# Gate and up projections of a SwiGLU block: seven Strassen-Winograd products in another order

## The chip, the cores and the metric

The kernel runs on one core of one Trainium2 chip. The metric is the time of one execution in microseconds (us), taken on the device; smaller is better. Before the change it is 1520.84 us, the median of three runs (1519.15 to 1520.98).

## The reference

One decoder block on 1024 positions of width 1024, in float32. Two mixers (stick-breaking attention and HGRN2) are merged into a residual h; then comes the part that the change touches, a feed-forward network with 2816 hidden channels:

```
hn = rms_norm(h, norm2_g)
ffn = (jax.nn.silu(hn @ w_gate) * (hn @ w_up)) @ w_down
return h + ffn
```

The result must be that of float32 arithmetic.

## The kernel before

Everything is kept transposed: channels lie on the 128 partitions, positions on the free axis, in two halves of 512. A float32 product is made of three matmuls on rounded parts: an operand is split into a high part (a cast, on ScalarE) and a low part (operand minus high part, on VectorE), and high by high, high by low and low by high are summed in one PSUM bank. `full_split` (line 860) issues the two instructions of a split. In the profile the high parts are called oh and the low parts ol.

The hidden channels are 22 tiles of 128. Tile p and tile p + 11 form a pair, and for each of the 11 pairs the gate and then the up are computed. Such a projection is a 2 by 2 block product: two tiles of channels by two halves of positions, with the 1024 input channels cut in two. It is done in Winograd's form with seven block products instead of eight. `left` (line 977) makes the seven left operands from two raw weight tiles, ta = (a11, a12) and tb = (a21, a22), of 512 KB each: operand 1 is a11, 2 is a12, 4 is a22; a21 = a11 - a21 is operand 7; s2 = a22 - a21 is operand 6; a11 = s2 + a11 is operand 5; a12 = a12 - s2 is operand 3. The sums are written back into the raw tiles (called w in the profile) or into s2. The right operands f are made once, earlier. `prod` (line 1002) issues one product: four steps of three matmuls, 12 matmuls in all, into one bank.

`winograd` (line 1028) issues the seven products into three banks and reads the banks in between, so that four output blocks come out: x (in the profile pj) sums products 1 and 2 and is block 0; y (ms) sums 6, 7 and 4; z sums 5 and 3. A copy p1 of product 1 is added to the others on VectorE: c[1] = 6 + 1 + 5 + 3, c[3] = 6 + 7 + 1 + 5, c[2] = 6 + 7 + 4 + 1. A bank that more products are to be added to is read before the next product writes it. For the first gate the order is another (1, 5, half of 2, 6, the channel sums of the norm, 7, rest of 2, 4, 3), since the right operands still come in; for the others it is 1, 6, 5, 7, 2, 4, 3. The blocks are called g in a gate and c in an up. A gate's blocks go through the norm's factor and silu; an up's are multiplied by them, four sums of the products are formed (bs), and all eight are stored for the down stage (act_d). `down_sums` makes four sums of the down weights in the same stage (ds, wd_d).

The instructions of this part are not issued in the order of the code. `Plan` (lines 74 to 211) collects them with a cost each, then goes through time in its own model: whenever an engine is free it takes the ready instruction with the longest way behind it, provided that its buffers have slots, and appends it to that engine's queue. A tile is followed as a whole: whoever writes one half of a raw tile stands in order with whoever reads the other half (lines 102 to 118). Products keep the order of the code (`after=(turn,)`). Loads go through SyncE's queue, in the order that the planner writes. The slots that matter: two raw tiles for a gate (w) and two for an up (wA), four split operands for each (oh and ol; ohA and olA, line 395), three banks each for x and y and two for z. A DMA is counted as landed 2.0 us after its transfer (line 87), a transfer as its KB divided by 350 (line 466).

On the chip each engine runs its queue in order and waits at an instruction until what it needs is there.

After this stage the down stage (from line 1115) multiplies the stored blocks with the down weights in the same form; the last outputs end the kernel.

Of the kernel before, what the change touches and what calls it, by code (L numbers as in the profile page):

```python
# [15 lines left out]
ALU = mybir.AluOpType  # L16
# [198 lines left out]
def hybrid_block(ctx: ExitStack, tc, xT, wi, wb, wo, wg, wu, wd, vec, outT):  # L215
# [213 lines left out]
    def new(ring, shape=(P, HALF), dt=F32):  # L429
        pool, cap, tag, phase = where[ring]  # L430
        plan.ring(ring, cap)

        def make():
            open_pools(phase)
            return (pools[pool] if phase else pool).tile(list(shape), dt, tag=tag, bufs=cap, name=tag)

        return Buf(ring, make, phase)
# [4 lines left out]
    def A(fn, *args, n=HALF, aps=0, rank=0, ps=False, part=False, holds=(), after=(), **kw):  # L442
        us = (0.05 if ps else 0.093) + n / 1200 + 0.0935 * aps
        return plan.op("A", us, [(fn, args, kw)], rank, after, part=part, holds=holds)

    def V(fn, *args, n=HALF, aps=0, rank=0, part=False, holds=(), after=(), **kw):
        cycles = 2 * n if fn == nc.vector.tensor_tensor_scan else n
        us = 0.067 + cycles / 960 + 0.061 * aps
        return plan.op("V", us, [(fn, args, kw)], rank, after, part=part, holds=holds)
# [15 lines left out]
    def L(dst, src, kb, rank=0, after=(), part=False, land=None):  # L465
        return plan.op("D", max(0.47, kb / 350), [(nc.sync.dma_start, (dst, src), {})], rank,
                       after, part=part, land=land)
# [5 lines left out]
    act, tt = nc.scalar.activation, nc.vector.tensor_tensor  # L473
# [40 lines left out]
    def load(dst, src, kb, rank=1):  # L514
        last_load[0] = L(dst, src, kb, rank=rank, after=(last_load[0],))
# [344 lines left out]
    def full_split(src, rings=("oh", "ol"), rank=0):  # L860
        hi, lo = new(rings[0], dt=F32R), new(rings[1], dt=F32R)
        A(nc.scalar.copy, hi, src, rank=rank)
        V(tt, lo, src, hi.bitcast(F32), op=ALU.subtract, rank=rank)
        return hi, lo
# [62 lines left out]
    for i in range(4):  # L927
# [6 lines left out]
        for e in range(2):  # L934
            k = i + 4 * e
            w = get_w(wo[seq.pop(0)])
            for h in range(2):
# [9 lines left out]
                y = new("f" if i < 3 else "y")  # L947
# [29 lines left out]
    def left(src, p, ring):  # L977

        A_ = "A" if ring == "wA" else ""
        sp = lambda t: full_split(t, ("oh" + A_, "ol" + A_))  # L980
        ta, tb = new(ring, (P, 1024)), new(ring, (P, 1024))
        for t, r in ((ta, src[p]), (tb, src[p + NP])):
            if A_:
                last_wu[0] = L(t, r, 512, after=(last_wu[0],))
            else:
                load(t, r, 512, rank=0)
        a11, a12, a21, a22 = ta[:, :512], ta[:, 512:], tb[:, :512], tb[:, 512:]
        s2 = new("s2")
        ops = {1: sp(a11)}
        V(tt, a21, a11, a21, op=ALU.subtract)  # L990
        V(tt, s2, a22, a21, op=ALU.subtract)
        ops[6] = sp(s2)
        V(tt, a11, s2, a11, op=ALU.add)
        ops[5] = sp(a11)
        ops[7] = sp(a21)
        ops[2] = sp(a12)
        ops[4] = sp(a22)
        V(tt, a12, a12, s2, op=ALU.subtract)
        ops[3] = sp(a12)
        return ops  # L1000

    def prod(out, a, p, start, ks=range(4)):

        nonlocal turn
        for k in ks:
            ws = slice(k * P, (k + 1) * P)
            turn = plan.op("P", 0.69, [
                (nc.tensor.matmul, (out, a[p][i][:, ws], fop[p][k][j]),
                 dict(start=start and k == 0 and i + j == 0, stop=k == 3 and i == 1,
                      skip_group_check=True)) for i, j in ((0, 0), (0, 1), (1, 0))], after=(turn,))  # L1010

    def channel_sums():

        nonlocal turn
        ss = []
        for h in range(2):
            hi, lo = new("bs", dt=F32R), new("bs", dt=F32R)
            A(nc.scalar.copy, hi, rs[h])
            V(tt, lo, rs[h], hi.bitcast(F32), op=ALU.subtract)
            ss.append(new("ms"))  # L1020
            turn = M(1024, [(ss[h], ones_r, hi, True, False), (ss[h], ones_r, lo, False, True)],
                     after=(turn,))
        for h in range(2):
            A(act, rs[h], ss[h], AF.Ln, n=HALF + (0 if h else TABLE), ps=True, aps=1, bias=eps_t, scale=1.0 / D)
        for h in range(2):
            A(act, rs[h], rs[h], AF.Exp, n=HALF + (0 if h else TABLE), scale=-0.5)

    def winograd(a, ring, first=False):

        c = [new(ring) for _ in range(4)]  # L1030
        x, y, z, p1 = new("pj"), new("ms"), new("z"), new("p1")
        prod(x, a, 1, True)
        A(nc.scalar.copy, p1, x, ps=True)
        if first:
            prod(z, a, 5, True)
            prod(x, a, 2, False, (0, 1))
            prod(y, a, 6, True)
            channel_sums()
            V(tt, c[1], y, p1, op=ALU.add)
            prod(y, a, 7, False)  # L1040
            prod(x, a, 2, False, (2, 3))
        else:
            prod(y, a, 6, True)
            V(tt, c[1], y, p1, op=ALU.add)
            prod(z, a, 5, True)
            prod(y, a, 7, False)
            prod(x, a, 2, False)
        V(tt, c[3], y, p1, op=ALU.add)
        V(tt, c[3], z, c[3], op=ALU.add)
        prod(y, a, 4, False)  # L1050
        V(tt, c[2], y, p1, op=ALU.add)
        prod(z, a, 3, False)
        V(tt, c[1], z, c[1], op=ALU.add)
        return x, c

    def down_sums(p):
# [10 lines left out]
        for b, t in enumerate((s7, s6, s5, s3)):  # L1067
            L(wdd[p][:, b * HALF:(b + 1) * HALF], t, 256, part=True)

    ag = left(wg, 0, "w")  # L1070
    for p in range(NP):
        au = left(wu, p, "wA")
        x, g = winograd(ag, "g", p == 0)
        V(tt, g[0], x, rs[0], op=ALU.mult)
        for b in range(1, 4):
            V(tt, g[b], g[b], rs[b % 2], op=ALU.mult)
        for b in range(4):
            A(act, g[b], g[b], AF.Silu, n=HALF + (0 if b or p else TABLE))
        for b in range(4):
            V(tt, g[b], g[b], rs[b % 2], op=ALU.mult)  # L1080
        down_sums(p)
        if p + 1 < NP:
            ag = left(wg, p + 1, "w")
        x, c = winograd(au, "c")
        V(tt, c[0], x, g[0], op=ALU.mult)
        for b in range(1, 4):
            V(tt, c[b], c[b], g[b], op=ALU.mult)
        n7, n6, n5, n4 = (new("bs") for _ in range(4))
        V(tt, n7, c[3], c[1], op=ALU.subtract)
        V(tt, n6, n7, c[0], op=ALU.add)  # L1090
        V(tt, n5, c[3], n6, op=ALU.subtract)
        V(tt, n4, c[2], n6, op=ALU.subtract)
        for b, t in enumerate((*c, n7, n6, n5, n4)):
            dst = actd[p][:, b * HALF:(b + 1) * HALF]
            store_a(dst, t) if p == NP - 1 else L(dst, t, 256, part=True)
# [33 lines left out]
    def operands(o, p):  # L1129

        wp = bp = dB
        tags, btags = ("ah", "al"), ("bh", "bl")
        if o == 1 and p < 4:

            rp = wpool if p < 2 else preB
            raw = rp.tile([P, 1024], F32, tag="w", bufs=2, name="w32")
            ra, rb = raw[:, :512], raw[:, 512:]
            if p < 3:
                wp = bp = rp
                tags = btags = ("oh", "ol") if p < 2 else ("ds", "ds")  # L1140
        else:
            ra = dB.tile([P, HALF], F32, tag="ra", name="ra")
            rb = dB.tile([P, HALF], F32, tag="rb", name="rb")
        nc.sync.dma_start(ra, LEFT[o](p))
        nc.sync.dma_start(rb, blk(act_d[p], RIGHT[o]))
        return split(ra, wp, tags) + split(rb, bp, btags)
# [17 lines left out]
    for o in DOWN:  # L1164
        first = o in (1, 6, 5)
        final = o == DOWN[-1]
        for p in range(NP - LAST if final else NP):
            ops = operands(o, p)
# [66 lines left out]
```

## Time and profile before

| | |
|---|---|
| median of three runs | 1520.84 us |
| the profiled execution: its time, its span | 1520.8 us, 1519.1 us |
| granted TensorE clock | 1.00 |
| TensorE busy (matmuls) | 1501.8 us, 99% |
| VectorE busy | 1194.1 us, 79% |
| ScalarE busy | 804.3 us, 53% |
| gate and up, from the first product to the first matmul of the down stage | 874.57 to 1305.93 us |

Times in the rows are microseconds from the start of the span unless they are marked ns. PE is TensorE's matmuls, PEld its weight loads, DVE VectorE, ACT ScalarE, SPq the queue of SyncE, which issues DMAs. A busy PE isn't a PE at its peak: matmuls overlap in the records, so the distance between the starts of two products tells more than the busy time. `out<-in` names what an instruction writes and reads; `[3.34 <-DMA w<-wu]` behind it is the idle time of its engine before it and what ended it. Nearly all instructions have line 194, that of the planner's call, so they are told apart by their tiles.

### The profile page before, as it was taken

How to read it: one execution, taken by the hardware profiler on the slowest of the kernel's cores; microseconds unless marked ns; L12 is line 12 of the kernel's file. 1: busy time of each engine (PE TensorE's matmuls, PEld its weight loads, DVE VectorE, ACT ScalarE, POOL GpSimd, SP SyncE). 2: the span in 40 equal slices, each digit the busy share in tenths (PEclk: the TensorE clock that was granted, in tenths of full speed). 3: DMA queues.
4: the chain of work that ended last, by engine and by line, in shares of the span. 5: the costliest groups of instructions: out<-in, count | busy, mean ns of one | idle time of the engine just before them, and what ended most of it. 6: DMA issues, size and time to landing. Idle time of an engine off the chain costs nothing.

```text
span 1519.1 us, 20504 instructions
## 1 busy us (share of the span) xinstructions
PE 1501.8 (99%) x7213; PEld 1238.3 (82%) x7213; DVE 1194.1 (79%) x2092; ACT 804.3 (53%) x1505; POOL 110.3 (7%) x155
## 2 busy tenths in 40 slices
PE   9999999999999999999999999999999999999999
PEld 6778888888888888888888888777888887888887
DVE  9898789988997877967867798788888888675553
ACT  7867779668758877445434453332332332354442
POOL 4210111211101100110000000000000000000000
PEclk9999999999999999999999999999999999999999
DMA  5111111111111212136434345444445544797662
GB/s 182 40 44 60 54 39 46 44 39 56 51 51 39 68 61 63 51 120 220 163 114 145 112 148 184 150 154 153 163 166 164 161 160 166 256 327 243 199 216 91
DMA packets 83159, 188.53 MB, mean 124 GB/s; under 512 B 9584, under 2 KB 11632, under 8 KB 83056
## 3 DMA queue, kind: packets, MB, share of 16 engines
q1 hardware_dynamic: 72400, 167.82, 34.2%
q10 hardware_dynamic: 10656, 19.40, 3.5%
q8 instruction: 57, 0.93, 0.3%
q14 instruction: 46, 0.38, 0.1%
HBM read 131.61 MB, written 55.57 MB: 123 GB/s over the span
## 4 chain that ended last, share of the span: by engine, by line
PE 69%; DVE 18%; DMA 5%; ACT 4%; issue 3%; POOL 1%; SPq 0%; DVEq 0%; ACTq 0%; POOLq 0%
PE pj L194 34%; PE f L1152 14%; PE ms L194 13%; PE z L194 8%; DVE ol L194 4%; DMA w<-wu 3%; DVE g L194 3%; DMA w<-wg 2%; DVE w L194 2%; DVE c L194 1%; DVE aa L194 1%; ACT aa L194 1%; ACT oh L194 1%; DVE kb L194 1%; DVE bs L194 1%
## 5 line engine op out<-in xcount | busy, mean ns | idle before, releaser
L194 PE MATMUL pj<-ah,oh 128*128 128x512 f32 x704 | 287.2, 408 | 2.4 <-ACT tmp L194 0.9
L194 PE MATMUL pj<-ah,ol 128*128 128x512 f32 x704 | 276.3, 393 | 0.0
L194 PE MATMUL pj<-al,oh 128*128 128x512 f32 x704 | 275.9, 392 | 0.0
L194 ACT CAST oh<-w 128x512 fp32r<-128x512 f32 x164 | 99.6, 619 | 237.3 <-DVE w L194 67.7
L194 DVE TENSOR_TENSOR ol<-w,oh 128x512 fp32r<-128x512 f32 x248 | 170.1, 686 | 31.0 <-ACT oh L194 23.5
L194 PE MATMUL ms<-f,oh 128*128 128x512 f32 x528 | 165.0, 394 | 3.1 <-DVE g L194 2.9
L194 PEld LDWEIGHTS pj<-ah,ol 128*128 128x128 f32 x704 | 132.6, 188 | 29.8
L194 PEld LDWEIGHTS pj<-ah,oh 128*128 128x128 f32 x704 | 132.9, 189 | 26.7 <-DVE aa L194 1.4
L194 PEld LDWEIGHTS pj<-al,oh 128*128 128x128 f32 x704 | 133.1, 189 | 23.1 <-DVE al L194 0.5
L194 PEld LDWEIGHTS ms<-f,oh 128*128 128x128 f32 x528 | 97.5, 188 | 29.5 <-DVE g L194 7.2
L1152 PE MATMUL f<-bh,ah 128*128 128x512 f32 x296 | 115.2, 389 | 0.0
L1152 PE MATMUL f<-bh,al 128*128 128x512 f32 x296 | 115.2, 389 | 0.0
L1152 PE MATMUL f<-bl,ah 128*128 128x512 f32 x296 | 115.1, 389 | 0.0
L194 DVE TENSOR_TENSOR_SCAN aa<-aa,ww 128x512 f32<-128x512 f32 (+3 forms) x96 | 94.2, 996 | 25.3 <-ACT aa L194 14.6
L194 PE MATMUL z<-f,oh 128*128 128x512 f32 x352 | 108.6, 390 | 0.0
L194 PE MATMUL pj<-f,oh 128*128 128x512 f32 x352 | 108.4, 389 | 0.0
L248 DVE TENSOR_TENSOR al<-ra,ah 128x512 fp32r<-128x512 f32 x73 | 50.4, 690 | 70.1 <-ACT ah L247 69.9
L194 PE MATMUL ms<-f,ol 128*128 128x512 f32 x264 | 102.9, 390 | 0.0
L194 POOL TENSOR_SCALAR oh<-w 128x512 fp32r<-128x512 f32 x84 | 68.4, 815 | 437.8 <-PE pj L194 367.7
L247 ACT CAST ah<-ra 128x512 fp32r<-128x512 f32 x73 | 45.5, 624 | 95.6 <-PE f L1152 83.8
L194 PE MATMUL pj<-mx,oh 128*128 128x512 f32 x256 | 78.7, 389 | 0.0
L194 PEld LDWEIGHTS pj<-f,oh 128*128 128x128 f32 x352 | 66.1, 188 | 13.7
(257 smaller groups left out, 3148.7 us busy)
## 6 DMA issues: line engine op xcount, KB each, us to landing
w<-wi SPq DMA_DIRECT2D x42, 512.0 KB, 3.6
rb<-act_d SPq DMA_DIRECT2D x73, 256.0 KB, 4.3
w<-wg SPq DMA_DIRECT2D x22, 512.0 KB, 4.3
w<-wu SPq DMA_DIRECT2D x22, 512.0 KB, 4.5
w<-wd SPq DMA_DIRECT2D x22, 512.0 KB, 5.0
wd_d<-ds SPq DMA_DIRECT2D x44, 256.0 KB, 2.8
ra<-wd_d SPq DMA_DIRECT2D x44, 256.0 KB, 4.1
act_d<-c SPq DMA_DIRECT2D x40, 256.0 KB, 4.2
```

The lines of the kernel that those rows point to most:

```text
L194: fn(*[a.real() if isinstance(a, View) else a for a in args], **{k: v.real() if isinstance(v, View) else v for k, v in kw.items()})
L247: pin(nc.scalar.copy(hi, src))
L248: pin(nc.vector.tensor_tensor(lo, src, hi.bitcast(F32), op=ALU.subtract))
L1152: nc.tensor.matmul(banks[SET[o]][d], l[:, ws], r, start=start and i == 0, stop=p == NP - 1 and i == 2, skip_group_check=True)
```

## The change

The order of products becomes 1, 6, 5, half of 2, 7, the rest of 2, 3, 4; for the first gate 1, 5, half of 2, 6, channel sums, 7, rest of 2, 3, 4. After product 5 its bank is read at once (c[3] = z + p1); the sum of y is added behind product 7. In `left`, the splits of operands 2 and 4 stand in that order too; where two instructions are otherwise equal the planner goes by this order.

```diff
         ops[5] = sp(a11)
+        ops[2] = sp(a12)
         ops[7] = sp(a21)
-        ops[2] = sp(a12)
-        ops[4] = sp(a22)
         V(tt, a12, a12, s2, op=ALU.subtract)
         ops[3] = sp(a12)
+        ops[4] = sp(a22)
         return ops
...
             prod(y, a, 6, True)
             channel_sums()
             V(tt, c[1], y, p1, op=ALU.add)
-            prod(y, a, 7, False)
-            prod(x, a, 2, False, (2, 3))
+            V(tt, c[3], z, p1, op=ALU.add)
         else:
             prod(y, a, 6, True)
             V(tt, c[1], y, p1, op=ALU.add)
             prod(z, a, 5, True)
-            prod(y, a, 7, False)
-            prod(x, a, 2, False)
-        V(tt, c[3], y, p1, op=ALU.add)
-        V(tt, c[3], z, c[3], op=ALU.add)
+            V(tt, c[3], z, p1, op=ALU.add)
+            prod(x, a, 2, False, (0, 1))
+
+        prod(y, a, 7, False)
+        V(tt, c[3], y, c[3], op=ALU.add)
+        prod(x, a, 2, False, (2, 3))
+        prod(z, a, 3, False)
+        V(tt, c[1], z, c[1], op=ALU.add)
         prod(y, a, 4, False)
         V(tt, c[2], y, p1, op=ALU.add)
-        prod(z, a, 3, False)
-        V(tt, c[1], z, c[1], op=ALU.add)
         return x, c
```

## Rows read from the trace of the kernel before

**Rows 1.** The page: span, and busy time, share and instructions of TensorE.
```profile
span 1519.1 us, 20504 instructions
...
PE 1501.8 (99%) x7213; PEld 1238.3 (82%) x7213; DVE 1194.1 (79%) x2092; ACT 804.3 (53%) x1505; POOL 110.3 (7%) x155
```

**Rows 2.** Stretches: first gate, first up, down stage; length, busy time by engine.
```profile
874.57:895.49 20.92, 20.59 (x89) 16.36 (x88) 20.80 (x35) 17.05 (x27) 0.00 (x0) 1.00 0.58 187
895.49:914.53 19.04, 19.04 (x85) 15.77 (x84) 15.87 (x27) 4.92 (x9) 0.00 (x0) 1.00 0.43 149
1305.93:1515.43 209.50, 209.49 (x925) 173.01 (x923) 120.30 (x189) 87.68 (x152) 0.00 (x0) 1.00 0.70 229
```

**Rows 3.** Stretches: products 5 and 7 of the ten later gates; then their sum.
```profile
919.97:925.43 5.46, 5.46 (x25) 4.49 (x24) 4.91 (x9) 1.22 (x2) 0.00 (x0) 1.00 0.81 248
958.59:965.91 7.32, 5.73 (x25) 4.42 (x24) 6.18 (x11) 1.21 (x2) 0.00 (x0) 1.00 0.80 259
999.14:1005.23 6.09, 5.73 (x25) 4.43 (x24) 4.96 (x9) 1.22 (x2) 0.00 (x0) 1.00 0.80 261
...
sum 59.89, PE 57.09 PEld 44.33 DVE 49.18 ACT 12.18 POOL 0.00; mean PE 5.71 PEld 4.43 DVE 4.92 ACT 1.22 POOL 0.00
```

**Rows 4.** Stretches: products 5 and 7 of the ten later ups; then their sum.
```profile
1018.83:1024.81 5.98, 5.88 (x25) 4.35 (x24) 5.48 (x10) 1.28 (x4) 0.00 (x0) 1.00 0.61 166
...
1136.14:1141.75 5.61, 5.61 (x26) 4.19 (x25) 5.10 (x9) 1.08 (x3) 0.00 (x0) 1.00 0.69 187
...
sum 59.21, PE 58.15 PEld 43.41 DVE 53.88 ACT 14.01 POOL 0.00; mean PE 5.81 PEld 4.34 DVE 5.39 ACT 1.40 POOL 0.00
```

**Rows 5.** Waits from 874 to 1306: who, for whom, total us, times, longest.
```profile
DVE w L194 <- DMA w<-wu: 30.6, 10, 4.6
...
PEld ms L194 <- DVE g L194: 7.2, 10, 2.0
PEld z L194 <- DVE ol L194: 4.9, 10, 0.7
...
PEld ms L194 <- DVE c L194: 2.3, 9, 0.3
```

**Rows 6.** VectorE in order of time, one pair: start, us, instruction, [idle before].
```profile
992.49 0.69 DVE L194 TENSOR_TENSOR w<-w 128x512 f32<-128x512 f32 x1 [3.34 <-DMA w<-wu]
...
1001.65 0.68 DVE L194 TENSOR_TENSOR g<-ms,p 128x512 f32<-128x512 f32 x1
1002.25 0.68 DVE L194 TENSOR_TENSOR ol<-w,oh 128x512 fp32r<-128x512 f32 x1
...
1007.86 0.69 DVE L194 TENSOR_TENSOR ol<-w,oh 128x512 fp32r<-128x512 f32 x1 [1.73 <-ACT oh L194]
...
1018.81 0.68 DVE L194 TENSOR_TENSOR ol<-w,oh 128x512 fp32r<-128x512 f32 x1
...
1021.82 0.68 DVE L194 TENSOR_TENSOR ol<-w,oh 128x512 fp32r<-128x512 f32 x1
...
1025.01 0.69 DVE L194 TENSOR_TENSOR c<-ms,p 128x512 f32<-128x512 f32 x1 [0.70 <-PE ms L194]
1025.62 0.68 DVE L194 TENSOR_TENSOR ol<-w,oh 128x512 fp32r<-128x512 f32 x1
```

**Rows 7.** The chain that ended last, two loads of it: start, us to landing.
```profile
987.06 5.41 DMA w<-wu
...
1002.95 4.17 DMA w<-wg
```

**Rows 8.** ScalarE in order of time, the last cast of that up.
```profile
1024.79 0.62 ACT L194 CAST oh<-w 128x512 fp32r<-128x512 f32 x1 [2.21 <-PE ms L194]
```

**Rows 9.** The tile wu: its 22 loads, issue to landing.
```profile
DMA to landing us min/median/max: 3.4/4.5/6.6
```

## The prediction

> **What bounds the kernel now.** The page first: the span is 1519.1 us and TensorE is busy for 99% of it [rows 1], so only lost TensorE time can be won back. The stretches by stage come next. The projections of gate and up run from 874.57 to 1305.93; the down stage behind them is 209.50 us of matmuls without a gap [rows 2], and the change touches nothing before 874. The up of the first pair runs clean: seven products in 19.04 us [rows 2], so a product is 2.72 us, half a product 1.36, and one of its twelve matmuls 0.227. That is the floor; everything above it is what a new order can win.
>
> Where it is lost: product 5 and the product 7 behind it should take 5.44 us together. Over the ten gates after the first they take 59.89 us, 5.49 more than ten times 5.44; in the worst pair 1.88, in a usual one 0.65 [rows 3]. Over the ten ups after the first they take 59.21, or 4.81 more [rows 4]. The first gate takes 20.92; less 19.04 and less four matmuls of channel sums (0.91) that is 0.97 [rows 2]. Together 11.27 us, and that is the most the change can give.
>
> Who is waited for: product 7 on VectorE's c[1] (called g in a gate), which reads the bank that product 7 writes next; product 5 of an up on the low half of its own left operand; and, briefly, product 7 of an up on c[1] [rows 5]. VectorE is late because its queue is in order: at 992.49 it has stood 3.34 us at a21 = a11 - a21, whose raw tile wu came 5.41 us after its issue at 987.06, and from there it takes a step every 0.60 us without a pause [rows 6, 7]. The planner counts 1.46 us for such a load and 2.0 for its landing, 3.46 together (lines 87 and 466), so the queue is written about 2 us too early at that place. The read of c[1] in the gate, due when product 6 ends at 999.14, starts at 1001.65 [rows 3, 6].
>
> **The change, part by part.** No instruction is added or taken: each product keeps its 12 matmuls, the number of VectorE sums stays five in a projection, and z + p1 stands where y + p1 stood, of the same shape. Only order changes, on TensorE, VectorE, ScalarE and, through them, SyncE.
>
> (1) *Half of product 2 goes between 5 and 7.* The read of y into c[1] gets 1.36 us more. Nine of the ten gates lose less than that: 5.49 - 1.88 = 3.61 us together, all of it gone. The worst keeps 1.88 - 1.36 = 0.52. So **-5.0** (bounds -5.5 and 0, where VectorE falls further behind). The cover is 4.08 us behind product 6; if VectorE reaches c[1] later than that, each us is paid once a gate.
>
> (2) *The bank of product 5 is read at once, product 7's sum later.* c[3] = z + p1 goes into VectorE's gap while product 2 runs; when product 7 ends only one sum of two is left, with 4.08 us until product 4 writes that bank (2.72 before). In the first gate the first wait, for c[1] behind the channel sums, stays; the ones behind it, about 0.4 of 0.97, go: **-0.4** (0 to -0.97).
>
> (3) *Product 3 ahead of 4.* c[1] + z, which in the profile comes in the steps behind the late raw tile, is ready one product earlier, and three sums of the output blocks hang on it. The planner places by due time, so one to three steps move from behind the blocked a21 into the 3.34 us that VectorE stands there [rows 6]. I take two, 1.2 us.
>
> (4) *The load behind it moves the other way.* The up has four slots for split operands (ohA, line 395). The planner follows whole tiles (line 105), so the splits of 2 and 5 wait for the sum written back into their tile, while 7 and 4 need only a21: in the up, slots go to 1, 7, 4 and 6, whatever order the lines stand in, and 5, 2 and 3 wait for products to end. The last cast of the up starts at 1024.79, when product 7 ends; its low half follows at 1025.62, and then the next raw tile is issued [rows 6, 8]. Product 7 now ends 1.36 us later within the up, and so does this load of SyncE. Two steps (1.2 us) come back by (3), so c[1] and the gate's raw tiles (wg, 4.17 us [rows 7]) stay where they were. From 1007.86, the first split of the next gate, to 1018.81, the low half of operand 5 of the up, VectorE goes on for 18 steps [rows 6]; the gate's slots also come 1.36 later, so its sums fill the time ahead of that split, and I take two steps fewer, 1.2 us.
>
> So operand 5 of the up: its low half is done at 1018.81 + 0.68 = 1019.49 and was due two matmuls into product 5, at 1018.83 + 0.45 = 1019.28 [rows 4, 6]; 0.2 late, and 0.65 more against a gate that no longer stalls. 0.85 + 1.36 - 1.2 - 1.2 = -0.2: just in time. The wait for c[1] in the up has 1.36 more cover and goes. With loads of 3.4 to 6.6 us [rows 9] some pairs stay late: I keep 1.5 of 4.81, so **-3.3** (bounds -4.8 and +8, where no step is won).
>
> (5) *What is late next.* Operand 2 of the up: its low half starts at 1021.82 [rows 6], done at 1022.50, and is now due two matmuls behind product 5, at 1018.83 + 2.72 + 0.45 = 1022.00. Late by 0.5 where VectorE is as far behind as now, in time when it is 0.6 ahead, as in (4). Operand 3 of the up: product 7 ends, its cast takes 0.6, its low half is done 1.5 us after that end (1024.79 to 1026.30 [rows 6, 8]); due 1.36 + 0.45 = 1.81. In time by 0.3, late by 0.3 with one VectorE step in front. Behind that wait stand the sums of c on VectorE and the raw tile on SyncE. I take half of one miss, 0.15, in eleven ups: **+1.6** (0 to 10, with both late by 0.9 together).
>
> Sum: -5.0 - 0.4 - 3.3 + 1.6 = -7.1 us. The profiled execution took 1520.8 (span 1519.1 and 1.7 around it), the same as the median of the three, 1520.84: **1513.7 us**.
>
> **Rivals.** *A: the wait only moves.* The pitch of a pair is then set by the round of raw tile, VectorE, raw tile, VectorE, not by the read of one bank. For it: between the two waits VectorE has no pause [rows 6], and a gate freed of its stall reaches the up sooner, where operand 5 isn't ready. Against it: in the sixth up the two products take only 5.61 [rows 4], so the round can close within 0.2 of the floor. With two to three steps won instead of four, (4) reads 0.85 + 1.36 - 1.2 (or 1.8) = 0.4 to 1.0 late in an up, with 0.3 for the restart 0.7 to 1.3 a pair, where 1.1 is lost now: -4 to +2 in ten pairs. Time 1520 (1517 to 1523). The Trainium skill has a rule on this side: Perfetto Trace Analysis, section Optimization Strategy, says that one gap repeating through a stretch on the engine that should be full can mean too few buffers for the next tile. By that rule four slots and two raw tiles would decide, the change gives neither, and the time stays. The trace agrees for the up (its casts wait for product ends) and not for the gate, where the wait ends on a read of a PSUM bank.
>
> *B: slower, by the raw tile.* The load in (4) is issued 1.36 us later in every up; if the planner puts no more in front of the blocked a21, all of VectorE's queue shifts by that, and operand 5 of the next up with it. Ten times 1.36 is 13.6 us; less one step in the gate's half, ten times 0.6, leaves +7.6: 1528.4. It decides from the point where fewer than two steps a pair move ahead of a load. For it: that product 7's end starts the cast is in the rows. Against it: the 3.3 us that VectorE stands idle there are room for five steps.
>
> *C: all of it goes.* If four or five steps move, no operand is late, and 11.3 us go less a little for long loads: 1510.0.
>
> **How the numbers follow.** Forecast 0.53 (1511.5 to 1517.5), C 0.18, A 0.18, B 0.11. Under about 0.2%, 3 us, a measurement of this kernel doesn't tell a change from none: faster is below 1517.8, slower above 1523.9. The forecast and C are faster, with a little of A: 0.73; the rest of A and a weak B are within: 0.17; B, and an A with an unlucky operand 3: 0.10. The range leaves out B and the floor: 1509.8 to 1521.0.
>
> **What would show it.** The order on TensorE is pj, ms, z, six matmuls of pj, ms, six of pj, z, ms. (1): no wait of product 7 on c[1] in the gates, or one. (3): the sum c from z stands ahead of a21 in VectorE's queue, and a21 has idled less than 3.3 us. (4): the load of wu behind an up's last cast is issued about 13.7 us (12.24 and 1.5) after that up's first matmul, 12.94 now; product 5 of the ups takes under 2.9 us. (5): a wait of z on a low half at product 3 of the ups under 0.3 us. From one up to the next 38.1 to 38.6 us, now 39.1. I'm wrong if that pitch stays, with the wait at product 5, 2 or 3 of the ups (A), or grows (B).

## The result, and the profile after

The changed kernel takes 1524.05 us (median of 14 runs, 1520.35 to 1528.37), the kernel before 1519.70 (14 runs beside them, 1517.78 to 1523.57): ratio 1.0026, 95% interval 1.0017 to 1.0035. It is slower by about 4 us, 0.3%; 1513.7 was forecast, and the range ended at 1521.0.

The page of the kernel after, span and TensorE, answers to [rows 1]; it counts the same instructions:

```profile
span 1523.0 us, 20504 instructions
...
PE 1499.3 (98%) x7213; PEld 1239.1 (81%) x7213; DVE 1195.0 (78%) x2092; ACT 803.8 (53%) x1505; POOL 112.0 (7%) x155
```

From the first gate to the down stage the trace after goes from 875.18 to 1308.00. Its first stretch is the first gate, its second the first up, as in [rows 2]:

```profile
875.18:895.64 20.46, 20.26 (x89) 16.44 (x88) 20.35 (x34) 16.44 (x26) 0.00 (x0) 1.00 0.60 191
895.64:914.68 19.04, 19.04 (x85) 15.77 (x84) 16.17 (x27) 5.49 (x10) 0.00 (x0) 1.00 0.47 154
```

The first gate has won 0.46. For [rows 3] and [rows 4] the stretch is now product 5, half of 2 and product 7, 6.80 us at the floor (2.72 + 1.36 + 2.72). First come three of the ten later gates of the kernel after, with the sum of all ten; then one of the ten later ups, with the sum of the ten:

```profile
997.84:1004.63 6.79, 6.79 (x31) 5.63 (x30) 5.01 (x9) 1.21 (x2) 0.00 (x0) 1.00 0.73 257
...
1074.09:1083.37 9.28, 7.41 (x32) 5.48 (x30) 8.12 (x14) 1.22 (x3) 0.00 (x0) 1.00 0.60 205
...
1193.89:1203.21 9.32, 7.39 (x32) 5.48 (x30) 8.17 (x14) 1.21 (x3) 0.00 (x0) 1.00 0.58 202
...
sum 80.29, PE 72.03 PEld 55.14 DVE 65.96 ACT 12.21 POOL 0.00; mean PE 7.20 PEld 5.51 DVE 6.60 ACT 1.22 POOL 0.00
```

```profile
1055.06:1061.85 6.79, 6.79 (x31) 5.63 (x30) 6.76 (x12) 1.50 (x3) 0.00 (x0) 1.00 0.36 114
...
sum 67.99, PE 67.99 PEld 56.30 DVE 63.39 ACT 15.07 POOL 0.00; mean PE 6.80 PEld 5.63 DVE 6.34 ACT 1.51 POOL 0.00
```

The ups lose nothing any more. The ten gates lose 80.29 - 68.00 = 12.29, where they lost 5.49 before; 1.55 of it is product 5 in the first two of them, waiting for its own low half. Who is waited for (after, 875 to 1306, columns as in [rows 5]):

```profile
DVE w L194 <- DMA w<-wu: 30.0, 10, 4.5
...
PEld ms L194 <- DVE g L194: 7.1, 8, 1.0
PEld pj L194 <- DVE ol L194: 5.9, 6, 1.7
...
PE pj L194 <- DVE ol L194: 3.6, 4, 1.3
...
PEld z L194 <- DVE ol L194: 1.8, 2, 1.0
```

The two lines of pj are new: the half of product 2 waits for the low half of its operand. Of the eight waits of PEld on g, that is on c[1], six come 1.8 us behind such a wait, in the same gates. TensorE in one such gate (after, order of time: start, us, instruction, [idle before]):

```profile
1076.81 0.61 PE L194 MATMUL pj<-f,oh 128*128 128x512 f32 x2
1078.70 0.50 PE L194 MATMUL pj<-f,ol 128*128 128x512 f32 x1 [1.27 <-DVE ol L194]
...
1080.50 0.73 PE L194 MATMUL ms<-f,oh 128*128 128x512 f32 x2 [0.61 <-DVE g L194]
```

And what VectorE does there (after, same columns):

```profile
1060.21 0.68 DVE L194 TENSOR_TENSOR c<-z,p 128x512 f32<-128x512 f32 x1
...
1069.57 0.69 DVE L194 TENSOR_TENSOR w<-w 128x512 f32<-128x512 f32 x1 [4.47 <-DMA w<-wu]
...
1072.89 0.69 DVE L194 TENSOR_TENSOR c<-z,c 128x512 f32<-128x512 f32 x1
...
1077.96 0.68 DVE L194 TENSOR_TENSOR ol<-w,oh 128x512 fp32r<-128x512 f32 x1
...
1079.16 0.69 DVE L194 TENSOR_TENSOR w<-w,s 128x512 f32<-128x512 f32 x1
1079.76 0.69 DVE L194 TENSOR_TENSOR g<-ms,p 128x512 f32<-128x512 f32 x1
```

The low half at 1077.96 is that of operand 2, since a12 = a12 - s2 at 1079.16 overwrites its tile. Before, in [rows 6], the same step of a gate (the kernel before):

```profile
999.84 0.69 DVE L194 TENSOR_TENSOR ol<-w,oh 128x512 fp32r<-128x512 f32 x1
```

It was done at 1000.52, and in the new order would have been due two matmuls behind product 5, at 999.14 + 2.72 + 0.45 = 1002.31: 1.8 in hand. After, it is done at 1078.64 and due at 1074.09 + 3.17 = 1077.26: 1.4 late.

The wait that ends last is another one. c[1] (the g of 1079.76) is done at 1080.45, 6.36 us after product 6 ended at 1074.09. The new order gives it 4.08, so it is 2.3 late, and 2.33 is what this gate loses ahead of product 7: without the wait for the low half, product 7 would have started no sooner, since VectorE's steps up to c[1] follow each other without a pause. So it is in all six gates that wait at the half of 2, each time to within 0.06 us; the low half is 0.9 less late than c[1]. In [rows 6] c[1] was done at 1002.33, 3.19 after product 6, with a cover of 2.72: 0.5 late. So the cover grew by 1.36, and the time until c[1] is done by 3.2.

Counted from the gate's first matmul (993.70 there, 1068.65 here, two pairs later) the low half has moved from 6.14 to 9.31, and c[1] by as much. Of those 3.2 us, 2.1 lie ahead of a21, which started 1.21 ahead of that matmul and now starts 0.92 behind it, after 4.47 us of idle time where [rows 6] have 3.34. The raw tile it waits for, on SyncE after and as the chain of waits has its load (start, us to landing):

```profile
1058.99 0.33 SPq L194 DMA_DIRECT2D w<-wu  x1
1060.32 1.53 SPq L194 DMA_DIRECT2D w<-wd  x2
1062.12 0.33 SPq L194 DMA_DIRECT2D w<-wu  x1
```

```profile
1062.12 7.42 DMA w<-wu
```

It was 5.41 in [rows 7]. In the last eight of the eleven ups both raw tiles are now fetched 3 us apart, with two tiles of down weights (wd) between them; before, they came 28 to 30 us apart in all but the first two ups.

One table holds the rest. Stage: from the first gate's first matmul to the second of the down stage; its floor is 154 products of 2.72 and 0.91 of channel sums, 419.8. Gates, ups: what the ten later gates and the eleven ups take above 19.04 each, from the starts of their products; one matmul of the down stage, 0.23, is in every figure of the stage and of the ups. Load, a21: when the raw tile that a21 waits for is issued, and when a21 starts, after the first matmul of the up before; medians of ten pairs. c[1]: when it is done in a gate, after the end of product 6, median of ten gates; its cover is 2.72, and 4.08 where half of 2 stands ahead of 7 (after, e2, e4, e5, e9, e11, e12). Times are medians, ratios against the runs of before on the same chip (its medians there 1519.1 to 1521.1).

| kernel | time | ratio, 95% interval | stage | gates | ups | load | a21 | c[1] |
|---|---|---|---|---|---|---|---|---|
| before | 1519.7 | 1 | 431.4 | 5.5 | 5.2 | 12.9 | 18.2 | 2.9 |
| after | 1524.05 | 1.0026, 1.0017 to 1.0035 | 432.8 | 12.3 | 0.2 | 12.3 | 18.9 | 5.0 |
| e1 | 1526.57 | 1.0036, 1.0022 to 1.0051 | 437.0 | 15.5 | 0.7 | 10.5 | 17.5 | 4.2 |
| e2 | 1524.18 | 1.0026, 1.0015 to 1.0036 | 436.3 | 1.1 | 15.0 | 15.3 | 19.7 | 2.8 |
| e3 | 1517.45 | 0.9982, 0.9971 to 0.9992 | 426.1 | 4.7 | 1.1 | 10.4 | 16.4 | 2.9 |
| e4 | 1517.51 | 0.9974, 0.9964 to 0.9985 | 426.7 | 6.1 | 0.2 | 12.3 | 17.8 | 4.4 |
| e5 | 1525.15 | 1.0040, 1.0026 to 1.0054 | 434.0 | 13.0 | 0.7 | 12.3 | 18.6 | 5.1 |
| e6 | 1519.65 | 1.0003, 0.9994 to 1.0012 | 428.2 | 4.6 | 3.3 | 10.8 | 16.5 | 2.8 |
| e7 | 1512.54 | 0.9959, 0.9946 to 0.9972 | 421.4 | 0.6 | 0.5 | 10.4 | 15.6 | 2.4 |
| e8 | 1511.57 | 0.9950, 0.9937 to 0.9962 | 421.3 | 0.0 | 0.5 | 12.4 | 16.0 | 1.4 |
| e9 | 1522.43 | 1.0011, 1.0000 to 1.0022 | 430.9 | 0.0 | 10.1 | 14.7 | 19.9 | 3.0 |
| e10 | 1516.07 | 0.9966, 0.9953 to 0.9979 | 423.8 | 0.5 | 2.9 | 10.8 | 16.0 | 2.4 |
| e11 | 1515.07 | 0.9957, 0.9941 to 0.9972 | 423.9 | 0.0 | 3.5 | 13.9 | 17.8 | 1.6 |
| e12 | 1519.10 | 0.9987, 0.9977 to 0.9997 | 427.8 | 6.9 | 0.7 | 12.4 | 18.0 | 4.8 |

The stages are of one execution each, and the stage holds only part of the 4 us. The two profiled spans differ by 3.9: 0.6 ahead of the stage, which the change doesn't touch, 1.4 in it, and 1.9 in the down stage (215.0 against 213.1), with TensorE waiting near its start. e5, of the same order but for 3 and 4, has 213.1 there and is as slow, so I count the 1.9 to that execution. Against before, the median times of the twelve experiments come out 1.5 below to 3.8 above what their stages say, 1.9 at the middle, so the stage of the profiled execution of before may be some 2 us longer than usual. Neither was tried by itself: where the rest of the 4 us lies is open.

### The profile page after: what moved, and what is told of

It reads as the page before. It is cut to its first block, busy times and chain, and to the rows that moved or that the text cites. A ratio compares the mean times of both kernels' runs of the same rounds, so it can differ in the third digit from the quotient of the medians.

```text
span 1523.0 us, 20504 instructions
## 1 busy us (share of the span) xinstructions
PE 1499.3 (98%) x7213; PEld 1239.1 (81%) x7213; DVE 1195.0 (78%) x2092; ACT 803.8 (53%) x1505; POOL 112.0 (7%) x155
## 4 chain that ended last, share of the span: by engine, by line
PE 74%; DVE 14%; DMA 4%; ACT 4%; issue 3%; POOL 1%; DVEq 0%; SPq 0%; ACTq 0%; POOLq 0%
PE pj L194 36%; PE ms L194 15%; PE f L1153 13%; PE z L194 9%; DVE ol L194 3%; DMA w<-wu 2%; DVE w L194 1%; DVE g L194 1%; DMA w<-wg 1%; DVE aa L194 1%; DVE c L194 1%; ACT aa L194 1%; DVE kb L194 1%; DVE bs L194 1%; DVE dl L194 1%
## 5 line engine op out<-in xcount | busy, mean ns | idle before, releaser
L194 PEld LDWEIGHTS z<-f,oh 128*128 128x128 f32 x352 | 66.1, 188 | 13.7
```

Source lines behind the costliest of these rows:

```text
L194: fn(*[a.real() if isinstance(a, View) else a for a in args], **{k: v.real() if isinstance(v, View) else v for k, v in kw.items()})
```

## Experiments

The first four set two theories against each other. S: the change makes the planner fill the ups' four slots and fetch the ups' raw tiles in another order (both together instead of 30 us apart), and that costs. O: the order of the products costs by itself.

**e1: the products of before, the slots of after.** In the ups the split of operand 4 waits until the cast of operand 5 (`last_cast[0]`) is issued.

```diff
         ops[5] = sp(a11)
+        five = last_cast[0]
...
-        ops[4] = sp(a22)
+        ops[4] = sp(a22, (five,) if A_ else ())
```

> The products in the order of the kernel before; only in the up operand 4 may not be split before operand 5, so the up's four slots go to 1, 7, 6, 5 as in the changed kernel, and both raw tiles of an up are loaded one right behind the other. Theory S (the time was lost because the two raw tiles of the up came to be loaded together, next to the down weights, and land late): wu tiles land 6 us and more after issue, a21 idles VectorE over 4 us, product 7 of the gates waits for c[1] 1.5 to 2.5 us more in each pair: 1523 to 1530 us, slower than before. Theory O (product 2 ahead of 7 needs its split earlier than VectorE can give it, whatever the loads): no change, 1519.7 us.

1526.57 us, a time that S wanted. The loss sits in the gates, at product 7 for c[1] (1.0 to 2.0 in eight of ten), and the ups are clean: the slots decide where the loss falls, and with the reads of before it is large. But it does not come about as S says. The raw tile lands 7.0 us after its issue at the median, yet it is issued 2.4 sooner than before, so a21 idles 2.3 and not over 4 and starts 0.7 sooner than before; c[1] is late because 17 steps of VectorE stand between the two, where before had 15.

**e2: the products of after, the slots of before.** In the ups the cast of operand 5 waits for those of 1, 6, 7 and 4 (kept in `casts`), that of 2 for that of 5.

```diff
-        ops[5] = sp(a11)
-        ops[2] = sp(a12)
         ops[7] = sp(a21)
+        ops[4] = sp(a22)
+        ops[5] = sp(a11, tuple(casts))
+        ops[2] = sp(a12, (casts[-1],))
...
-        ops[4] = sp(a22)
```

> The changed order of products; in the up operand 5 may not be split before 7, 4 and 6, so the slots go to 1, 7, 4, 6 as in the kernel before and one raw tile of the next up is loaded some 30 us ahead. This is the state in which the prediction was worked out. Theory S: gates lose under 1 us in all, the ups some; 1513 to 1518 us, faster than before. Theory O: product 2 still waits for its low half in the gates; 1523 us and more.

1524.18 us: S alone is wrong. O has the time right but not the place, since the gates lose only 1.1. These are the slots on which the prediction was worked out, and TensorE waits at product 5 of the ups (e2, order of time):

```profile
1057.07 0.61 PE L194 MATMUL z<-f,oh 128*128 128x512 f32 x2
1059.08 0.50 PE L194 MATMUL z<-f,ol 128*128 128x512 f32 x1 [1.39 <-DVE ol L194]
```

**e3: the early read alone.** Order 1, 6, 5, 7, 2, 4, 3; c[3] = z + p1 ahead of product 7.

```diff
             V(tt, c[1], y, p1, op=ALU.add)
+            V(tt, c[3], z, p1, op=ALU.add)
             prod(y, a, 7, False)
             prod(x, a, 2, False, (2, 3))
...
             prod(z, a, 5, True)
+            V(tt, c[3], z, p1, op=ALU.add)
             prod(y, a, 7, False)
             prod(x, a, 2, False)
-        V(tt, c[3], y, p1, op=ALU.add)
-        V(tt, c[3], z, c[3], op=ALU.add)
+        V(tt, c[3], y, c[3], op=ALU.add)
```

> Products in the order of the kernel before; only the bank of product 5 is read at once (c[3] = z + p1 before product 7). By the planner's rules the slots of the up then also go to 1, 7, 6, 5. Theory S: slower than before by 3 us or more, like the run with forced slots. Theory O: within 0.2% of before, since no product moved.

1517.45 us, faster than before by 0.2%, and not slower as S wanted. The early read alone also brings the ups' raw tiles together (e3, SyncE):

```profile
1057.31 0.33 SPq L194 DMA_DIRECT2D w<-wd  x1
...
1059.12 0.33 SPq L194 DMA_DIRECT2D w<-wu  x1
1059.72 0.33 SPq L194 DMA_DIRECT2D w<-wd  x1
1060.92 0.33 SPq L194 DMA_DIRECT2D w<-wu  x1
```

So loads 2 us apart are no loss by themselves: the last one (at the median of the ten pairs) is issued 10.4 us after the up's first matmul, not 12.9, and a21 starts 1.8 sooner.

**e4: the changed kernel, the loads of the down weights held** until both raw tiles of the next up are issued (one edit of order on SyncE; nothing is left out).

```diff
-            last_wd[0] = L(t, r, 512, after=(last_wd[0],))
+            last_wd[0] = L(t, r, 512, after=(last_wd[0], last_wu[0]))
```

> The changed kernel, but the two loads of down weights of a pair wait until both raw tiles of the up are issued. Theory S: the second raw tile lands 4 to 5 us after issue instead of 6 to 7.4, a21 idles VectorE about 2.5 us instead of 4.5, and product 2 of the gates waits under 0.5 us: 1514 to 1518 us. Theory O: no change against the changed kernel, 1523 to 1525 us.

1517.51 us, as S wanted: 6 us of stage come back. The raw tile is issued as late as in after (12.3) but lands 5.5 us after its issue at the median, not 6.3, and lets a21 start 1.1 sooner. S had wanted a landing of 4 to 5 us, and the gates still lose 6.1.

**e5: the changed kernel with 4 ahead of 3 again.**

```diff
-        prod(z, a, 3, False)
-        V(tt, c[1], z, c[1], op=ALU.add)
         prod(y, a, 4, False)
         V(tt, c[2], y, p1, op=ALU.add)
+        prod(z, a, 3, False)
+        V(tt, c[1], z, c[1], op=ALU.add)
```

> The changed kernel with product 4 ahead of 3 again; the half of product 2 ahead of 7 and the early read stay. Theory H (the half of product 2 ahead of 7 makes the gate's low half of operand 2 due 2.72 us sooner than it can be made, and that is what the change lost against its early read): the exchange of 3 and 4 is worth nothing, 1522 to 1527 us, ratio to before 1.001 to 1.004, and the first half of product 2 of the gates still waits 0.7 to 2.4 us per pair for its low half. Theory X (the exchange of 3 and 4 costs, because product 4 at the end of a step leaves its two sums to run beside the first sums of the next): 1515 to 1519 us and no such wait. The prediction's own step on the exchange (two VectorE steps, 1.2 us, moved into the idle time) would make this kernel slower than the change: over 1527 us.

1525.15 us, the time of after, with its waits: the exchange is not the cause. As in after, c[1] is the wait that ends last: in nine of the ten gates the loss ahead of product 7 is what c[1] is late, to within 0.06 us, and the low half of operand 2 is 1.5 less late.

**e6: the changed kernel with product 2 whole, behind 7.**

```diff
-            prod(x, a, 2, False, (0, 1))
...
-        prod(x, a, 2, False, (2, 3))
+        prod(x, a, 2, False, (2, 3) if first else range(4))
```

> The changed kernel with the whole of product 2 behind 7 (order 1, 6, 5, 7, 2, 3, 4, early read kept). Theory H: the wait at product 2 of the gates goes, because its low half is due 2.72 us later, and the time is that of the early read alone: 1515.5 to 1519.5 us, ratio 0.996 to 0.9995, stage of eleven gates and eleven ups near 426 us. Theory X: the exchange stays and so does the loss: 1522 to 1527 us. Prediction's theory (the half ahead of 7 saves 5 us in the gates): without it product 7 waits again for its low half or for the bank, some 0.5 us per gate, 1526 to 1530 us.

1519.65 us, just above what H wanted, with an interval that holds 1. The wait at product 2 is gone and the gates lose 4.6. H's reason is not the one that the trace shows, though: c[1] is due 1.36 us sooner here than in after, and loses less because it is done at 2.8 and not at 5.0. The load is issued 1.5 sooner and a21 starts 2.4 sooner. The ups lose 3.3, which e3 didn't; what the exchange does to them is not settled.

**e7: e3 with the edit of e4.**

> The order of products of before, the early read of bank 5, and the loads of the down projection's weights held until both raw tiles of the next up are issued. If the two effects add (early read about 5 us of the stage against before, loads no longer beside the raw tile up to 6 us): 1511 to 1515 us, ratio 0.994 to 0.997, no VectorE wait on a raw tile over 3 us. If the stage with the early read is already near its floor, 154 products of 2.72 us each, 419.8 us with the last refill, and its leftover waits are not the raw tile's: 1516 to 1519 us, as with the early read alone.

1512.54 us, in the range for two effects that add: e4's edit takes another 4.7 us of stage off e3, and the stage is 1.6 above its floor. But e8 below has as short a stage without the early read, so with the wd loads held the early read adds nothing.

**e8: the kernel before with the edit of e4, one line.**

> The kernel before with only the loads of the down projection's weights held until both raw tiles are issued: a control. If these loads cost only where both raw tiles are fetched together, as in the changed kernel: no change, 1518.5 to 1522 us, ratio 0.999 to 1.001. If they delay the raw tile in before just as much (its landing 4.5 us at the median against 3.5 for the gate's): 1513 to 1517 us, ratio 0.996 to 0.998, and the VectorE wait on the raw tile falls from 4.6 us to under 4.

1511.57 us, the lowest median of all (its interval overlaps with that of e7), and better than its hopeful expectation. This was meant as a control. SyncE and a21 in one pair of the kernel before, then of e8:

```profile
1060.73 0.33 SPq L194 DMA_DIRECT2D w<-wd  x1
...
1062.53 0.33 SPq L194 DMA_DIRECT2D w<-wd  x1
...
1065.73 0.33 SPq L194 DMA_DIRECT2D w<-wu  x1
...
1070.83 0.69 DVE L194 TENSOR_TENSOR w<-w 128x512 f32<-128x512 f32 x1 [3.00 <-DMA w<-wu]
```

```profile
1061.63 0.33 SPq L194 DMA_DIRECT2D w<-wu  x1
1062.01 0.90 SPq L194 DMA_DIRECT2D w<-wd  x2
...
1065.19 0.69 DVE L194 TENSOR_TENSOR w<-w 128x512 f32<-128x512 f32 x1 [1.48 <-DMA w<-wu]
```

From issue to a21: 5.10 us with two wd loads of 512 KB issued 5.0 and 3.2 us ahead, 3.56 with them behind. Its waits and landings in e8 (before: 30.6 [rows 5] and 4.5 [rows 9]):

```profile
DVE w L194 <- DMA w<-wu: 15.9, 10, 2.2
...
DMA to landing us min/median/max: 3.5/3.6/4.4
```

No product of the ten gates waits any more, and of the ups only one by over 0.25. Nearly all that the change could win lay here, 10.1 of 11.6 us of stage, with the order of products untouched.

**e9: the half of product 2 alone, in the kernel before.**

```diff
+            prod(x, a, 2, False, (0, 1))
             prod(y, a, 7, False)
-            prod(x, a, 2, False)
+            prod(x, a, 2, False, (2, 3))
```

> The kernel before with one part of the change alone: the first half of product 2 of the gates and ups between 5 and 7, no early read, 4 ahead of 3. The slots of its left operands stay as in before (1, 7, 4, 6 together in the ups). The prediction's step on the half of product 2 (the gates lose 5.0 us of waits and nothing else moves): 1513 to 1516 us, ratio 0.996 to 0.998. Theory H (the half makes low half of operand 2 due 2.72 us sooner in a kernel whose raw tile comes late, so the wait moves): 1519 to 1525 us, ratio 1.000 to 1.004, waits at the first half of product 2 in the gates or at product 5 of the ups of 0.5 us or more per pair.

1522.43 us, within 0.2% of before. Its raw tiles still come 30 us apart (SyncE: 1036.16 and 1065.49), the slots are those of before. The gates are clean, with c[1] at 3.0 under a cover of 4.08, and what they lost is lost in the ups, 10.1 against 5.2, at product 5 (e9, waits, then order of time):

```profile
PEld z L194 <- DVE ol L194: 10.3, 9, 1.5
PE z L194 <- DVE ol L194: 6.4, 9, 1.1
```

```profile
1057.45 0.50 PE L194 MATMUL z<-f,ol 128*128 128x512 f32 x1 [0.70 <-DVE ol L194]
```

**e10: e6 with the edit of e4.**

> The changed kernel without the half of product 2 ahead of 7, and with the loads of the down projection's weights held until both raw tiles of the next up are issued. Theory D (the weights' loads ahead of or beside the raw tile are the source of nearly all stalls of the gates and ups, and the half of 2 is the only part of the change that costs with them gone): stage 421 to 422.5 us, 1511 to 1513.5 us, ratio 0.995 to 0.9965. If the exchange of 3 and 4 costs by itself (the early read alone 0.9982, with the exchange 1.0003): 1514 to 1517 us.

1516.07 us and a stage of 423.8: what was wanted where the exchange costs by itself (2.4 of stage against e7). With the half it costs nothing (e5 to after -1.2, e12 to e4 -1.1); why is open.

**e11: e2 with the edit of e4.**

> The changed kernel with the slots of the ups forced back to the order of before (1, 7, 4, 6 together, as in the run that forced them alone, 1524 us), and the weights' loads held behind both raw tiles. Theory D: the raw tile was this kernel's trouble too, 1511 to 1514 us. Rival T (in that order operand 5 of the ups is late through ScalarE's casts and the freed slots, not through the raw tile): product 5 of the ups keeps most of its 1.7 to 1.9 us per pair, 1520 to 1525 us.

1515.07 us, a little above D's range. T is wrong: with the raw tile landing in 3.7 us at the median instead of 4.9, product 5 of the ups loses 3.3 instead of 13.3. Where operand 5 is late, VectorE's lateness behind a21 is most of the reason; the slots place the loss, since e4 and e12, with other slots, lose next to nothing in the ups.

**e12: e5 with the edit of e4.**

> The changed kernel with 4 ahead of 3 again and the weights' loads held behind both raw tiles: what the half of product 2 costs with the tile on time, without the exchange. The change with the held loads took 1517.5 us (0.9974), the early read with them 1512.5 us (0.9959). If the half costs by being due 2.72 us sooner whatever the tile does: 1516 to 1520 us, ratio 0.997 to 1.000, with 0.4 to 1.0 us of waits at product 2 of the gates per pair. If it costs only with a late tile: 1511 to 1514 us.

1519.10 us: with less of the raw tile's lateness the half still costs (6.4 of stage against e7). The load itself comes later, 12.4 against 10.4, and c[1] is done at 4.8 against 2.4: the half buys 1.36 of cover and costs 2.4. As in e5, the low half of operand 2 is 1.5 less late than c[1].

## Why the prediction was wrong

**The bound held.** The stage was 11.6 above its floor, and ten of it could go: e7 and e8 leave 1.6 and 1.5. That VectorE's order behind a late raw tile makes these waits was right too; e4, e7, e8, e10, e11 and e12 each differ from their partner only by e4's edit and by what the planner makes of it, and all six win 4 to 12 us of stage.

**(1), -5.0 in the gates, measured +6.8 (5.49 to 12.29).** The rule held: a gate loses what c[1] is late beyond its cover, and in e9, on the slots of before, every one of the waits went. The size failed. The term sets the new cover of 4.08 against the lateness of [rows 6], 3.2 in that pair and 2.9 at the median; in the changed kernel c[1] is done at 5.0 at the median. The step's own last sentence, that each us beyond 4.08 is paid once a gate, is what happened: six gates pay 0.75 to 2.33 for c[1], 9.4 together, and some 0.2 each while TensorE starts again; with the 1.55 at product 5 that makes the 12.29. The bound of 0 for a VectorE that falls further behind left it out. (5) looked for a late operand 2 in the ups alone; in the gates its low half is late too, but always less than c[1].

**(2), -0.4: measured -0.46.** Right in the first gate, and the early read alone does it: e3 and e7 show the same 20.46 or 20.47. That the early read would change the order in which the ups' raw tiles are fetched (e3) was not seen.

**(3), two steps into the idle time: not in the changed kernel.** c[1] from z stands behind a21 (1072.89 against 1069.57), and a21 idles 4.47 rather than less than 3.34. In e9, without the exchange, the idle time did shrink, from about 3.0 to 1.6 at the median, and 13 steps instead of 15 stand between a21 and c[1].

**(4) is the step that failed**, where it says that by (3) two steps come back for the load that goes out later, so that c[1] and the gate's raw tiles "stay where they were". No step came back and c[1] did not stay. At the median a21 started 1.4 us ahead of the gate's first matmul and now starts 0.1 ahead, 16 steps instead of 15 stand between it and c[1], and c[1] is done 2.1 us later against product 6. The half alone moves the load by more than the 1.36 of the step: by 1.8 us from before to e9 (12.9 to 14.7), and by 1.5 to 2.0 in the other four pairs of kernels that differ by the half alone (e3 and e5, e6 and after, e7 and e12, e10 and e4); a21 follows by 1.7 to 2.4. Why the planner moves the load by more than 1.36 is open. In the changed kernel the early read pulls the load ahead as well (10.4 in e3), so it goes out at 12.3, not at the 13.7 that I put. But between the wd loads and behind the other raw tile it lands 6.3 us after its issue at the median, where before had 5.3, and a21 starts 0.7 later in the up, which is half a us shorter now.

The same step says that slots go "to 1, 7, 4 and 6, whatever order the lines stand in", and makes from it operand 5 of the up "-0.2: just in time". In the changed kernel the loads stand otherwise, and the ups lose nothing, which is -5.0 where I put -3.3. That this term had the right sign is luck: where the slots do stand as I had them, the ups lose more than before, 10.1 in e9 (product 5 loses 0.7 to 1.4 in nine of eleven) and 15.0 in e2 (mostly 1.3 to 2.4).

**(5), +1.6 in the ups: measured 0.** Neither operand 2 nor operand 3 is late there.

By terms, in the profiled executions: +6.8 - 0.5 - 5.0 = +1.4 of stage, where -7.1 was forecast. The pitch from up to up was to be 38.1 to 38.6; it is 38.1 and 38.2 in two early pairs and up to 40.6 later.

Two readings of the rows were wrong and changed little. The "usual" gate that loses 0.65 was that of one pair; the median of the ten is 0.35. And the stretch of the sixth up [rows 4] begins 0.16 us late, since its product 5 starts at 1135.98 (before, TensorE):

```profile
1135.98 0.61 PE L194 MATMUL z<-f,oh 128*128 128x512 f32 x2
```

So the two products take 5.77 there and not 5.61, the ups lose 4.95 and not 4.81, and what stood against rival A, a round within 0.2 of the floor, was one within 0.33.

**The rivals.** A, that the wait only moves, is what e9 measures (stage -0.5, time 1522.4, inside A's 1517 to 1523). B is what the half shows: with it the raw tile is issued later (12.3 in after, 10.8 in e6), no step moves ahead of the blocked a21, and VectorE's queue goes late with it. I priced B at 1528.4 and gave it 0.11. It came out at 1524, because the ups won what B had them lose, while the gates paid. A needed two or three steps won, B fewer than two; the step count was the weak point, and the range should have reached B. The Trainium skill's rule that I set beside A (Perfetto Trace Analysis, Optimization Strategy: one repeating gap can mean too few buffers) doesn't describe this gap: in e8 the number of buffers is unchanged and the gap is gone. The Trainium skill's page DMA: Bandwidth & Descriptors (Issuing engines are not separate DMA queues) says that DMAs run on the same 16 DMA engines and interleave, whichever engine starts them. The 5.10 us from issue to a21 behind two other loads, and 3.56 ahead of them, agree with it; they would agree as well with loads of one queue that wait for those ahead of them, and no run here tells the two apart.

**What I passed over.** I read the late raw tile in [rows 6, 7] as given, and weighed only how its lateness would be passed on. What made it late was one view away: the queue of SyncE shows two 512 KB loads issued 3 to 5 us ahead of the one that everything waits for; e8 puts them behind it, and no product of the gates waits.

## What to carry to other kernels

When an in-order engine stands at a late load, new orders of the work behind it mostly move the stall: half of product 2 ahead of 7 won nothing in any of its four kernels without the edit (after, e2, e5, e9), the early read won 0.2%, and one line that held other loads back won 0.5%. Ask first which other loads are issued just ahead of the one that is late. When work is moved forward, write down what else is issued later by it, above all the load that the next round waits for. And where two waits follow each other, work out for each when it would end without the other: the one that shows as new needn't be the one that costs.

## What was not expected of the hardware

The same 512 KB load of a raw tile landed in 3.4 to 3.6 us at best in every kernel, and in 7.4 at worst, with two others of that size issued within 2 us of it (after, e1). Holding the wd loads moves the cost to them, where nobody waits: their median is 6.4 in e8, 5.0 before.
